# A two-layer transformer block: one more group by sevens in four down blocks, its combinations made earlier, and residuals added by transfers

## The chip, the cores and the metric

The kernel runs on one core of one Trainium2 chip. The metric is the device time of one execution in microseconds, lower is better. A core has five engines that run side by side, each with its own queue in order: TensorE (PE; its weight loads are shown as PEld), VectorE (DVE), ScalarE (ACT), GpSimd (POOL) and SyncE (SP). SP issues the plain loads, POOL the transfers that add to what lies at their destination; all run on 16 DMA engines.

## The reference

Two layers on 256 tokens of width 2048, each a mixer and an FFN. The change touches the FFN alone:

```python
def swiglu(hn, w_gate, w_up, w_down):
    return (jax.nn.silu(hn @ w_gate) * (hn @ w_up)) @ w_down

    for layer in range(DEPTH):
        ...
        h = h + swiglu(rmsnorm(h, ffn_norm[layer]), ffn_w_gate[layer], ffn_w_up[layer], ffn_w_down[layer])
    return rmsnorm(h, final_norm)
```

The FFN's inner width is 5632. Everything is float32. The kernel splits each operand of a matmul into a high part of type `F32R` and a rest of the same type, and a product is three matmuls: high by high, high by rest, rest by high.

## The kernel before

The inner width is cut into 11 pieces of 512 columns, and these into pieces of four, four and three. Each piece is first made by its gate/up blocks, one per 512 columns (called G0, G1, G2 and, in pieces of four, G3), and then used by two down blocks (D0, D1), each of which makes 1024 of the 2048 output columns for this piece. So a layer has 17 blocks, all written by `block` (L418).

A block multiplies 256 tokens (two halves `t`) by weights that come in units of 256 rows by 512 columns, 512 KB each. `load` (L166) has SP fetch a unit into a `raw` buffer. ScalarE casts the high part (`whi`, L179) and VectorE subtracts (`wlo`, L180). A unit is then 12 matmuls of 512 columns (lines L409 to L411), which add up in four PSUM banks `F[t][i]`.

Four units (two of rows, two of columns) make a group. A group that is done plainly takes 48 matmuls. A group in `comb` is done by sevens, which is Strassen's scheme in Winograd's form: the generator `seven` (L433) makes seven products of 6 matmuls in place of eight. For it, VectorE makes three sums of units (`total`, L384). ScalarE and VectorE split four tiles more (`halves`, L376 and L377). One sum is made by an adding load that POOL issues (L443). The tokens' side needs sums as well: `combine` (L387) makes them with VectorE and ScalarE, once per group and for all blocks that use it. At the end, `ends` (L460) recombines the products from the banks `M` into the buffer `e` (ScalarE at L462, four VectorE operations at L464).

Which groups go by sevens before the change: in gate/up blocks none or two of the four (`groups`); in D0 the first, in D1 of the pieces of four the first two, in D1 of the last piece the first. The combinations of `hid` for the down blocks are made by hooks: a hook `j` of a block runs before its plain unit `j`. In a piece of four, D0 makes the first at hook 4 and the second at hook 9. In the piece of three, G1 makes the only one at hook 6. `lead` says how many plain units come before the steps of the sevens begin to be mixed in.

At the end of a gate/up block VectorE and ScalarE form silu(gate) times up (L529 to L534). The result is transposed by TensorE in the next block's hook 2 (`turn`, L498), where ScalarE and VectorE write `hid` (L507, L508). At the end of a down block VectorE first makes `h +- e` in `e` (L554), which needs no accumulator, and then adds the four banks `F` to it into `h` (L561).

The order on each engine is not the code's: a planner sorts all instructions by the code's order as priority and by its own costs, so an instruction whose inputs are there can come tens of microseconds earlier than it is written. The buffers set how far an engine runs ahead: seven `raw` tiles, four `whi`, three `wlo`, two each of `thi`, `tlo` and `T`, four accumulator banks `F`, and one buffer `e`.

Of the kernel before, what the change touches and what calls it, by code (L numbers as in the profile page):

```python
# [16 lines left out]
NB = FF // 512  # L17
# [30 lines left out]
def body(tc, A, out):  # L48
# [364 lines left out]

    def sums():

        return [[mx.tile([128, 512], F32, name=f"e{t}{i}", tag=f"e{t}{i}", bufs=1) for i in range(2)] for t in range(2)]

    def block(src, x, comb, nd, hooks, tail=0, lead=2, trail=None):  # L418

# [38 lines left out]
            yield  # L458

        def ends():  # L460
            (c1, w5), (v, w7) = sums()
            S.copy(c1, M[0].t)  # L462
            for o, a, b, op in ((v, M[2], c1, ALU.subtract), (w5, M[1], v, ALU.add), (v, M[3], v, ALU.add), (w7, M[3], w5, ALU.add)):
                V.tensor_tensor(out=o, in0=a.t, in1=b, op=op)  # L464
            return [[c1, w5], [v, w7]]

        sevens = [s for m in comb for s in [seven(m)] for _ in range(7)]
        trail = trail or (3 if ns == 1 and nd > 3 else 2)
# [2 lines left out]
        for j, (i, u) in enumerate(plain):  # L471
# [14 lines left out]
            while k < len(sevens) and k < (j - lead + 2) * len(sevens) // gaps:  # L486
                next(sevens[k])
                k += 1
                if k == len(sevens):
                    e = ends()  # L490
        return [[y.t for y in f] for f in F], e

    def ffn(L, then, fin=None):

# [17 lines left out]
        for groups in ((0, 2, 2, 2), (2, 2, 2, 2), (2, 2, 2)):  # L512
            piece = len(groups)
            hid = ogp.tile([128, 16, 2, T], F32R, name="hid", tag="hid")
            late = {4: lambda hid=hid: ch.update({0: combine(hid[:, 0:4])})}
            for j in range(piece):
                hooks = {2: turn} if todo else {}
                if b == 0:
                    hooks[5] = lambda: cx.update({0: combine(X[:, 0:4])})
                    hooks[8] = rstd  # L520
                    hooks[10] = lambda: cx.update({1: combine(X[:, 4:8])})
                if j == 1 and piece == 3:

                    hooks[6] = late[4]
                F, e = block(lambda i, u: gu[b, u, i], lambda k: X[:, k], {m: lambda m=m: cx[m] for m in range(groups[j])}, 4, hooks)
                a = e or sums()
                for t in range(2):
                    if e:
                        V.tensor_tensor(out=a[t][0], in0=F[t][0], in1=e[t][0], op=(ALU.add, ALU.subtract)[t])  # L529
                    S.activation(a[t][0], a[t][0] if e else F[t][0], AF.Silu, scale=nrm["rs"][:, t:t + 1])  # L530
                for t in range(2):
                    if e:
                        V.tensor_tensor(out=a[t][1], in0=F[t][1], in1=e[t][1], op=ALU.add)
                    V.scalar_tensor_tensor(out=a[t][0], in0=a[t][1] if e else F[t][1], scalar=nrm["rs"][:, t:t + 1],  # L534
                                           in1=a[t][0], op0=ALU.mult, op1=ALU.mult)
                    todo.append((hid, j, t, a[t][0]))
                b += 1
            u0 = 2 * (b - piece)
            for p in range(2):
                end = b == NB and p == 1  # L540
                hooks = {2: turn} if todo else {}
                if p == 0 and piece == 4:
                    hooks.update(late)

                    hooks[9] = lambda hid=hid: ch.update({1: combine(hid[:, 4:8])})
                if end and fin:
                    hooks.update({5: lambda: then(0), 6: lambda: then(1)})
                last = (3, 1, 3) if end and fin else (0, 5 if 4 in hooks else 2)
                F, e = block(lambda i, u: dn[2 * p + i, u0 + u], lambda k: hid[:, k],
                             {m: lambda m=m: ch[m] for m in range(1 + (p == 1 and piece == 4))}, piece, hooks, *last)  # L550
                hs = [[h[:, t, (2 * p + i) * 512:(2 * p + i + 1) * 512] for i in range(2)] for t in range(2)]
                for t in range(2):
                    for i in range(2):
                        V.tensor_tensor(out=e[t][i], in0=hs[t][i], in1=e[t][i], op=ALU.subtract if t > i else ALU.add)  # L554
# [743 lines left out]
```

## Time and profile before

| | |
|---|---|
| median of 3 runs (lowest, highest) | 2227.39 us (2226.42, 2228.13) |
| the profiled execution | 2228.4 us, span 2226.6 us |
| granted clock of TensorE | 0.999 of full speed |
| TensorE busy | 2211.8 us, 99% of the span |
| VectorE busy | 1917.1 us, 86% |
| ScalarE busy | 1284.9 us, 58% |
| HBM reads | 447.58 MB |

The times in the rows are of the one profiled execution. Busy time counts an engine's compute instructions; where two of them overlap in the pipeline, the stretch counts once. One matmul is shown with the time that it takes from its start to its modelled end, and the next starts before that end. So the pace is read from the starts. Register, semaphore and issuing instructions are not busy time. A layer's FFN lies from about 440 to 1130 us (layer 0) and from about 1530 us to the end (layer 1).

### The profile page before, as it was taken

How to read it: one execution, taken by the hardware profiler on the slowest of the kernel's cores; microseconds unless marked ns; L12 is line 12 of the kernel's file. 1: busy time of each engine (PE TensorE's matmuls, PEld its weight loads, DVE VectorE, ACT ScalarE, POOL GpSimd, SP SyncE). 2: the span in 40 equal slices, each digit the busy share in tenths (PEclk: the TensorE clock that was granted, in tenths of full speed). 3: DMA queues.
4: the chain of work that ended last, by engine and by line, in shares of the span. 5: the costliest groups of instructions: out<-in, count | busy, mean ns of one | idle time of the engine just before them, and what ended most of it. 6: DMA issues, size and time to landing. Idle time of an engine off the chain costs nothing.

```text
span 2226.6 us, 30372 instructions
## 1 busy us (share of the span) xinstructions
PE 2211.8 (99%) x11002; PEld 1847.0 (83%) x11002; DVE 1917.1 (86%) x2713; ACT 1284.9 (58%) x1687; POOL 50.6 (2%) x62
## 2 busy tenths in 40 slices
PE   9999999999999999999999999999999999999998
PEld 8888888888888888888878888888888888888886
DVE  8899676679999999999966658866999999999998
ACT  6776664555555665555654444545665566555565
POOL 0000000000000000000000000000000000000000
PEclk9999999999999999999999999999999999999999
DMA  7445445677777776777665455556777777777774
GB/s 281 155 146 163 141 152 184 208 223 227 212 227 231 220 233 211 225 230 225 193 196 171 161 169 175 168 178 185 223 226 216 221 225 238 219 214 239 218 236 151
DMA packets 125992, 451.67 MB, mean 203 GB/s; under 512 B 14065, under 2 KB 15601, under 8 KB 125713
## 3 DMA queue, kind: packets, MB, share of 16 engines
q1 hardware_dynamic: 117488, 420.10, 58.3%
q0 software_dynamic: 8064, 29.36, 7.8%
q8 instruction: 86, 1.41, 0.3%
q14 instruction: 66, 0.53, 0.1%
q10 hardware_dynamic: 288, 0.27, 0.0%
HBM read 447.58 MB, written 2.10 MB: 202 GB/s over the span
## 4 chain that ended last, share of the span: by engine, by line
PE 95%; DVE 2%; issue 1%; ACT 1%; DMA 1%; DVEq 0%; ACTq 0%
PE F L411 15%; PE F L410 15%; PE F L409 15%; PE Pw L199 10%; PE Pw L204 5%; PE Px L303 5%; PE Px L304 5%; PE Px L305 5%; PE M L410 5%; PE M L411 4%; PE M L409 4%; PE Ph L503 1%; DVE wlo L180 1%; PE Psc L1068 1%; PE Pt L326 0%
## 5 line engine op out<-in xcount | busy, mean ns | idle before, releaser
L179 ACT CAST whi<-raw 128x1024 fp32r<-128x1024 f32 x720 | 755.3, 1051 | 666.8 <-PE F L411 263.8
L180 DVE TENSOR_TENSOR wlo<-raw,whi 128x1024 fp32r<-128x1024 f32 x720 | 874.5, 1219 | 189.3 <-PE Px L304 70.1
L199 PE MATMUL Pw<-X,whi 128*128 128x512 f32 x1088 | 388.3, 400 | 0.0
L409 PE MATMUL F<-whi,X 128*128 128x512 f32 x848 | 331.4, 391 | 0.0
L410 PE MATMUL F<-wlo,X 128*128 128x512 f32 x848 | 330.4, 390 | 0.0
L411 PE MATMUL F<-whi,X 128*128 128x512 f32 x848 | 330.0, 389 | 0.0
L204 PE MATMUL Pw<-X,wlo 128*128 128x256 f32 x1088 | 304.8, 280 | 1.0 <-DVE wlo L180 0.9
L376 ACT CAST thi<-T 128x1024 fp32r<-128x1024 f32 x168 | 176.6, 1051 | 124.1 <-DVE T L384 84.0
L199 PEld LDWEIGHTS Pw<-X,whi 128*128 128x128 f32 x1088 | 204.2, 188 | 47.7 <-issue 0.5
L377 DVE TENSOR_TENSOR tlo<-T,thi 128x1024 fp32r<-128x1024 f32 x168 | 205.1, 1221 | 28.0 <-ACT thi L376 27.3
L204 PEld LDWEIGHTS Pw<-X,wlo 128*128 128x128 f32 x1088 | 205.3, 189 | 2.4 <-DVE wlo L180 2.0
L409 PE MATMUL F<-whi,hid 128*128 128x512 f32 x480 | 187.5, 391 | 0.0
L411 PE MATMUL F<-whi,hid 128*128 128x512 f32 x480 | 186.9, 389 | 0.0
L410 PE MATMUL F<-wlo,hid 128*128 128x512 f32 x480 | 186.8, 389 | 0.0
L411 PEld LDWEIGHTS F<-whi,X 128*128 128x128 f32 x848 | 159.2, 188 | 33.1
L409 PEld LDWEIGHTS F<-whi,X 128*128 128x128 f32 x848 | 159.2, 188 | 32.7
L410 PEld LDWEIGHTS F<-wlo,X 128*128 128x128 f32 x848 | 159.2, 188 | 32.4
L384 DVE TENSOR_TENSOR T<-T,raw 128x1024 f32<-128x1024 f32 x112 | 136.5, 1219 | 1.1 <-DMA raw<-in_gu 0.2
L410 PE MATMUL M<-tlo,comb 128*128 128x512 f32 x336 | 131.8, 392 | 1.1 <-DVE tlo L377 1.0
L409 PE MATMUL M<-thi,comb 128*128 128x512 f32 x336 | 131.4, 391 | 0.0
L411 PE MATMUL M<-thi,comb 128*128 128x512 f32 x336 | 130.9, 390 | 0.0
L411 PEld LDWEIGHTS F<-whi,hid 128*128 128x128 f32 x480 | 90.1, 188 | 18.8
(389 smaller groups left out, 3409.5 us busy)
## 6 DMA issues: line engine op xcount, KB each, us to landing
raw<-in_gu SPq DMA_DIRECT2D x352, 512.0 KB, 4.4
raw<-in_dn SPq DMA_DIRECT2D x176, 512.0 KB, 4.4
raw<-in_w0w SPq DMA_DIRECT2D x72, 512.0 KB, 3.6
raw<-in_wo SPq DMA_DIRECT2D x64, 512.0 KB, 3.6
raw<-in_w1w SPq DMA_DIRECT2D x64, 512.0 KB, 3.6
raw<-in_gu POOLq DMA_DIRECT2D x40, 512.0 KB, 6.8
raw<-in_w1x SPq DMA_DIRECT2D x32, 512.0 KB, 3.7
raw<-in_w0x SPq DMA_DIRECT2D x16, 512.0 KB, 3.6
```

The lines of the kernel that those rows point to most:

```text
L179: S.copy(hi, raw)
L180: V.tensor_sub(lo, raw, hi.bitcast(F32))
L199: PE.matmul(P.rearrange("p a b -> p (a b)"), hi[:, kk], X[:, k].rearrange("p a b -> p (a b)"), start=k == 0, stop=False)
L204: PE.matmul(P[:, 0], lo[:, kk], X[:, k, 0], start=False, stop=k == NK - 1)
L303: PE.matmul(Ps[t], x[:, 0, ts], hi[:, kk], start=k == 0, stop=False)
L304: PE.matmul(Ps[t], x[:, 0, ts], lo[:, kk], start=False, stop=False)
L376: S.copy(hi, t)
L377: V.tensor_sub(lo, t, hi.bitcast(F32))
L384: V.tensor_tensor(out=t, in0=a, in1=b, op=ALU.add)
L409: PE.matmul(self.t, xh, hi[:, kk], start=self.i == kk == 0, stop=False)
L410: PE.matmul(self.t, xh, lo[:, kk], start=False, stop=False)
L411: PE.matmul(self.t, xl, hi[:, kk], start=False, stop=kk == 1 and self.i == self.n - 1)
```

## The change

In the pieces of four, D0 gets its second group by sevens, as D1 had it. Both combinations are now made in the gate/up blocks: the first at hook 6 of G2, the second at hook 6 of G3 (`chs`). D0 then has no hook 4, so its `lead` becomes 2, the value that D1 has. In all down blocks but those of the last piece (`b < NB`) the residual is no longer added by VectorE: it adds the banks `F` to `e`, and POOL issues two transfers that add the halves of `e` onto `h` in SBUF, 512 KB each. For this the four tiles of `e` become one tile of the same size.

```diff
     def sums():
-        return [[mx.tile([128, 512], F32, name=f"e{t}{i}", tag=f"e{t}{i}", bufs=1) for i in range(2)] for t in range(2)]
+        e = mx.tile([128, 2, 2, 512], F32, name="e", tag="e", bufs=1)
+        return [[e[:, t, i] for i in range(2)] for t in range(2)], e
...
         def ends():
-            (c1, w5), (v, w7) = sums()
+            ((c1, w5), (v, w7)), e = sums()
...
-            return [[c1, w5], [v, w7]]
+            return [[c1, w5], [v, w7]], e
...
-            late = {4: lambda hid=hid: ch.update({0: combine(hid[:, 0:4])})}
+            both = piece == 4
+            chs = lambda m, hid=hid: lambda: ch.update({m: combine(hid[:, 4 * m:4 * m + 4])})
...
-                if j == 1 and piece == 3:
-                    hooks[6] = late[4]
+                if j == 1 and piece == 3 or j == 2 and both:
+                    hooks[6] = chs(0)
+                if j == 3 and both:
+                    hooks[6] = chs(1)
...
-                if p == 0 and piece == 4:
-                    hooks.update(late)
-                    hooks[9] = lambda hid=hid: ch.update({1: combine(hid[:, 4:8])})
+                if p == 0 and piece == 4 and not both:
+                    hooks[4] = chs(0)
+                    hooks[9] = chs(1)
...
-                             {m: lambda m=m: ch[m] for m in range(1 + (p == 1 and piece == 4))}, piece, hooks, *last)
+                             {m: lambda m=m: ch[m] for m in range(1 + (both or p == 1 and piece == 4))}, piece, hooks, *last)
...
+                if b < NB:
+                    for t in range(2):
+                        for i in range(2):
+                            V.tensor_tensor(out=e[t][i], in0=F[t][i], in1=e[t][i], op=ALU.subtract if t > i else ALU.add)
+                        G.dma_start(h[:, t, 2 * p * 512:(2 * p + 2) * 512], es[:, t].rearrange("p a b -> p (a b)"), accum_op=ALU.add)
+                    continue
```

## Rows read from the trace of the kernel before

**Rows 1.** The page of the whole span: its length, and the busy time, the share of the span and the instructions of TensorE and VectorE.

```profile
span 2226.6 us, 30372 instructions
...
PE 2211.8 (99%) x11002; PEld 1847.0 (83%) x11002; DVE 1917.1 (86%) x2713; ACT 1284.9 (58%) x1687; POOL 50.6 (2%) x62
```

**Rows 2.** Busy time of each engine in eight stretches, each one block of an FFN layer, cut where the last VectorE instruction of the block before and of this block ends. Columns: stretch (us), its length, then busy us and instructions of PE, PEld, DVE, ACT and POOL, the granted clock, the share of the 16 DMA engines' time in use, GB/s. In order: layer 0's first piece of four, G3, D0 and D1; G0 of its second piece; G0 and G1 of its last piece; layer 1, G0 of the second piece and G0 of the last.

```profile
564.90:607.00 42.10, 42.02 (x189) 34.33 (x188) 41.03 (x46) 24.65 (x27) 0.95 (x2) 1.00 0.70 223
607.00:646.70 39.70, 39.70 (x181) 32.97 (x180) 37.57 (x44) 21.44 (x23) 1.64 (x2) 1.00 0.73 209
646.70:688.00 41.30, 41.30 (x184) 34.15 (x183) 38.57 (x40) 22.55 (x24) 0.96 (x2) 1.00 0.77 231
688.00:730.10 42.10, 42.10 (x186) 34.29 (x185) 39.84 (x40) 24.84 (x26) 2.49 (x3) 1.00 0.81 233
938.50:982.90 44.40, 43.64 (x193) 35.56 (x192) 41.94 (x42) 26.68 (x28) 2.48 (x3) 1.00 0.79 228
982.90:1024.80 41.90, 41.90 (x191) 34.76 (x190) 40.96 (x46) 25.24 (x28) 1.73 (x2) 1.00 0.73 217
1780.00:1822.40 42.40, 42.17 (x186) 34.23 (x185) 39.88 (x41) 24.90 (x26) 2.57 (x3) 1.00 0.80 230
2031.00:2074.20 43.20, 43.20 (x192) 35.48 (x191) 41.96 (x42) 26.51 (x28) 2.50 (x3) 1.00 0.80 233
```

**Rows 3.** TensorE's matmuls in order of time in that D1; first and last of 33 that follow each other. Columns: start, duration, engine, line, operation, output and inputs, shape, count.

```profile
654.74 0.39 PE L410 MATMUL F<-wlo,comb 128*128 128x512 f32 x1
...
662.00 0.39 PE L409 MATMUL M<-thi,comb 128*128 128x512 f32 x1
```

**Rows 4.** Who waited for whom over the whole span, weight loads of TensorE: total us, times, longest.

```profile
PEld M L410 <- DVE tlo L377: 4.0, 8, 1.2
```

**Rows 5.** VectorE's instructions in order of time at the start of that G3 (columns as in group 3; x2 merges two that follow each other).

```profile
559.46 0.68 DVE L529 TENSOR_TENSOR e<-F,e 128x512 f32<-128x512 f32 x1
560.06 0.68 DVE L533 TENSOR_TENSOR e<-F,e 128x512 f32<-128x512 f32 x1
...
567.12 2.35 DVE L180 TENSOR_TENSOR wlo<-raw,whi 128x1024 fp32r<-128x1024 f32 x2
569.39 1.22 DVE L384 TENSOR_TENSOR T<-T,raw 128x1024 f32<-128x1024 f32 x1
...
576.27 1.22 DVE L392 TENSOR_TENSOR cf<-hid 128x1024 f32<-128x1024 f32 x1
```

**Rows 6.** Groups of instructions by line, engine, operation and shape over the whole span: count, busy us, mean ns of one, idle time of the engine before them and what ended it.

```profile
L376 ACT CAST thi<-T 128x1024 fp32r<-128x1024 f32 x168 | 176.6, 1051 | 124.1 <-DVE T L384 84.0 <-PE F L410 23.1 <-PE F L411 14.3
...
L554 DVE TENSOR_TENSOR e<-h,e 128x512 f32<-128x512 f32 x48 | 31.2, 682 | 0.0
```

**Rows 7.** VectorE's instructions in order of time in G1 of layer 0's last piece, parts of one combination: its first operation (L392), two of its four small ones (L395) with what follows each.

```profile
994.28 1.22 DVE L392 TENSOR_TENSOR cf<-hid 128x1024 f32<-128x1024 f32 x1
...
1009.50 0.41 DVE L395 TENSOR_TENSOR cc<-cf 128x256 f32<-128x256 f32 x1
1009.83 1.21 DVE L377 TENSOR_TENSOR tlo<-raw,thi 128x1024 fp32r<-128x1024 f32 x1
...
1014.23 0.87 DVE L395 TENSOR_TENSOR cc<-cf,cc 128x256 f32<-128x256 f32 x2
1015.29 1.23 DVE L180 TENSOR_TENSOR wlo<-raw,whi 128x1024 fp32r<-128x1024 f32 x1 [0.19 <-PE F L410]
```

**Rows 8.** The DMA view of the whole span: packets, MB and share of the 16 engines' time of the two queues (q1 is what SP issues, q0 what POOL issues), then issues with the engine that issues, their count, KB each and median us from issue to landing.

```profile
q1 hardware_dynamic: 117488, 420.10, 58.3%
q0 software_dynamic: 8064, 29.36, 7.8%
...
raw<-in_dn SPq DMA_DIRECT2D x176, 512.0 KB, 4.4
...
raw<-in_gu POOLq DMA_DIRECT2D x40, 512.0 KB, 6.8
...
raw<-in_dn POOLq DMA_DIRECT2D x16, 512.0 KB, 7.3
```

**Rows 9.** ScalarE's instructions in order of time: in the D1 at 646.7 the first that writes the block's buffer `e`, in the G0 at 688.0 the one that reads the sum that the adding load made.

```profile
667.79 0.58 ACT L462 COPY e<-M 128x512 f32<-128x512 f32 x1
...
700.35 1.06 ACT L376 CAST thi<-raw 128x1024 fp32r<-128x1024 f32 x1 [0.79 <-PE M L411]
```

**Rows 10.** POOL's instructions in order of time around that D1, and in G0 of layer 0's last piece: each issues one adding load.

```profile
641.04 0.86 POOL L443 DMA_DIRECT2D raw<-in_dn  x1 [33.26 <-DVE T L384]
656.93 0.86 POOL L443 DMA_DIRECT2D raw<-in_dn  x1 [15.03 <-ACT thi L376]
687.90 0.86 POOL L443 DMA_DIRECT2D raw<-in_gu  x1 [30.11 <-ACT whi L179]
700.08 0.86 POOL L443 DMA_DIRECT2D raw<-in_gu  x1 [11.32 <-ACT thi L376]
...
950.57 0.86 POOL L443 DMA_DIRECT2D raw<-in_gu  x1 [11.32 <-ACT thi L376]
```

**Rows 11.** The chain of work that ended last, in order of time, two pieces of it in G0 of layer 0's last piece: start, us, what.

```profile
951.20 9.00 DMA raw<-in_gu
960.28 1.06 ACT whi L179
```

**Rows 12.** Who waited for whom over the whole span, ScalarE for weight loads of gate and up.

```profile
ACT whi L179 <- DMA raw<-in_gu: 18.4, 15, 2.1
```

More of the change, by code (lines that the diff above doesn't have):

```diff
@@ L490, in block @@
                     e = ends()
-        return [[y.t for y in f] for f in F], e
+        return [[y.t for y in f] for f in F], *(e or (None, None))
     def ffn(L, then, fin=None):
@@ L521, in ffn @@
                     hooks[10] = lambda: cx.update({1: combine(X[:, 4:8])})
-                if j == 1 and piece == 3:
-                    hooks[6] = late[4]
-                F, e = block(lambda i, u: gu[b, u, i], lambda k: X[:, k], {m: lambda m=m: cx[m] for m in range(groups[j])}, 4, hooks)
-                a = e or sums()
+                if j == 1 and piece == 3 or j == 2 and both:
+                    hooks[6] = chs(0)
+                if j == 3 and both:
+                    hooks[6] = chs(1)
+                F, e, _ = block(lambda i, u: gu[b, u, i], lambda k: X[:, k], {m: lambda m=m: cx[m] for m in range(groups[j])}, 4, hooks)
+                a = e or sums()[0]
                 for t in range(2):
@@ L548, in ffn @@
                 last = (3, 1, 3) if end and fin else (0, 5 if 4 in hooks else 2)
-                F, e = block(lambda i, u: dn[2 * p + i, u0 + u], lambda k: hid[:, k],
-                             {m: lambda m=m: ch[m] for m in range(1 + (p == 1 and piece == 4))}, piece, hooks, *last)
+                F, e, es = block(lambda i, u: dn[2 * p + i, u0 + u], lambda k: hid[:, k],
+                             {m: lambda m=m: ch[m] for m in range(1 + (both or p == 1 and piece == 4))}, piece, hooks, *last)
                 hs = [[h[:, t, (2 * p + i) * 512:(2 * p + i + 1) * 512] for i in range(2)] for t in range(2)]
+                if b < NB:
[4 more added lines that the diff above has]
+                    continue
                 for t in range(2):
```

## The prediction

> **What bounds the kernel now.** I read the page's busy times first [rows 1]: TensorE 99% of the span and VectorE 86%, so the order of these two decides. Then I cut the two FFN layers into blocks at the end of each block's last VectorE instruction and read the busy times block by block [rows 2]. Call a piece's gate/up blocks G0 to G3 and its down blocks D0 and D1. TensorE is busy in all of a D0 (39.70 of 39.70 us) and of a D1 (41.30 of 41.30), at a granted clock of 1.00, the 2.4 GHz level. VectorE is close behind: 37.57 us in a D0, 38.57 in a D1, 41.03 in a G3. So a matmul taken away is worth its own time only as long as VectorE, which gets work in exchange, stays under TensorE. The third view is the matmuls in order of time [rows 3]: 32 starts of 128x512 between 654.74 and 662.00 us, 0.2269 us each. This pace, and not the 0.39 us of one, prices a matmul. A fourth view, who waited for whom, says what TensorE loses to VectorE in all: the largest entry is 4.0 us in 8 waits of the weight load on `tlo` [rows 4]. So hardly more than the matmuls themselves is there to be won.
>
> **Part 1, the second group by sevens.** A plain group of D0 is 4 units of 12 matmuls, 48; by sevens it is 7 steps of 6, 42. Four D0 blocks (two per layer) lose 6 each: 24 x 0.2269 = 5.45 us, all on the engine that is never idle there. This is the whole gain.
>
> What pays for it. On VectorE a plain group is 4 subtractions (L180); by sevens it is 3 of these, 4 of L377 and 3 sums of L384, 10 in all, so 6 more. Two 1024-element instructions back to back start 1.135 us apart (567.12 and 569.39 are two apart [rows 5]), so a D0 gets 6.8 us more. ScalarE gets 3 more casts of 1.05 us (L376 [rows 6]) and is busy in 21.44 of a D0's 39.70 us [rows 2], so that is hidden. Loads stay 16 per block (12+4 becomes 8+8), and there is one more adding load (L443).
>
> **Part 2, the combinations move** from D0 (hooks 4 and 9) to hook 6 of G2 and G3. One `combine` is two 1024-element operations (2.27 us) and four of 256, 0.33 us apart where one is followed by another engine's input and 0.43 where they are in a chain [rows 7]: 3.8 us. The count stays, so this is a question of place. The order in the trace is not the order in the code: the first operation on `hid` runs at 576.27 [rows 5], in a G3, though the code puts it in the D0 whose window begins at 607.0. So G3 carries a combination already and only G2 gets a new one. VectorE's need in a gate block with two groups by sevens: 28 operations of 1.135 us (31.8), 10 of 512 elements at 0.60 (559.46 to 560.06 [rows 5]) for the recombination, the end and the turn, two scaled ones of about 0.66, together 39.1 us. TensorE needs 180 x 0.2269 + 0.9 for the 8 transposes, 41.7. With a combination VectorE needs 42.9, 1.2 more than TensorE has. Bounds: nothing, because G1 of a last piece, which has a combination at hook 6 and two groups by sevens, shows TensorE busy for 41.90 of 41.90 us [rows 2]; and 1.2 us in each of the eight G2 and G3, 9.6 us, if no tile is ready ahead. I take the nearest rows: idle 0.08 us in the G3 (42.10 less 42.02) and nothing in that G1, mean 0.04. With the new D0, which has the form of such a gate block, that is eight blocks, four G2 and four D0: 0.3 us. The start of D0 loses the three extra plain units that `lead` 5 gave; the turn at hook 2 then has 42 matmuls ahead of it in place of 24, which is more cover, not less.
>
> **Part 3, the residual.** In the eight down blocks of the pieces of four, the four operations `h +- e` (L554, 682 ns [rows 6], 0.60 in a row) go: 2.4 us of VectorE per block. The four after the last matmul stay, with `e` as their output in place of `h`, so accumulator banks come free when they did. D0's VectorE need becomes 28 x 1.135 + 10 x 0.60 = 37.8 us for 41.7 of TensorE. So D0 stays under TensorE by 3.9 us, and over a layer VectorE has 2 x 6.8 - 4 x 2.4 = 4.0 us more while rows 2 show 0.9 to 2.7 us idle in each block. What VectorE saves here gives no time back by itself, because it isn't the bound there.
>
> In place of these come two additions of 512 KB from SBUF onto `h` per block end, 16 in all, on the POOL queue. The trace has none of this kind. The nearest is the adding load L443: 7.3 us to landing, against 4.4 for a plain load [rows 8]. In time of all 16 engines: queue 0 took 7.8% of 2226.6 us for 29.36 MB, so 3.1 us per 512 KB; queue 1 took 58.3% for 420.10 MB, 1.62 us. A D1 then has 16 x 1.62 + 2 x 3.1 = 32.1 us of transfers in 41.3, 0.78; the row says 0.77. With two additions it is 38.3, 0.93. So it fits on average, and it is tight for some 12 us after each block end.
>
> Who waits for that? The buffer `e` is written again by the next block's L462, at 667.79 for a D0 that ended at 646.7 [rows 9]: 21 us, against two issues of 0.86 and two additions, 7.3 + 3.1. `h` is read next in the last piece. Behind the additions on the POOL queue stands the next block's adding load. From D0 to D1 the first is issued at 641.04, before D0's end, and the second at 656.93; from D1 to G0 at 687.90 and 700.08 [rows 10], the first of them just when the additions become ready. If it comes behind them it is late by up to 2 x 0.86 + 6.2 = 7.9 us; its reader at 700.35 [rows 9] leaves 12.4 less the 6.8 to landing [rows 8], 5.6. And the weight loads beside them become slow: in a G0 the chain of waits passes through a load of 9.00 us that was issued just behind an adding load [rows 10, 11], and TensorE is idle in that block for 0.76 us (44.40 less 43.64 [rows 2]). The four G0 that follow a D1 give 0, 0.76, 0.23 and 0: mean 0.25 us. Bounds for a block end: less than nothing is possible (VectorE has 2.4 us less to do there, which could take away the idle time of the four G0, 0.99 in all); from above, two additions' 6.2 us less what is ready ahead (the second rival). I take the mean of the four rows, since these are the blocks in which adding loads stand closest: 8 x 0.25 = 2.0 us.
>
> The Trainium skill, DMA: Bandwidth & Descriptors, section Issuing engines are not separate DMA queues, speaks against this part: what is issued from GpSimd runs on the same 16 engines as SP's loads and interleaves with them. By that the additions are no free path, and the 9.00 us load agrees. The Trainium skill's fit for one transfer (same title, section Anatomy of one DMA), 2.0 us and the bytes by 436 GB/s, would give 3.2 us for an addition, an estimate; by it the 2.0 us above would be nothing and the sum 2222.2. The adding loads here took 6.8 and 7.3 [rows 8], so the fit does not hold in this crowd.
>
> **The sum.** -5.45 + 0.3 + 2.0 = -3.15 us. The profiled execution took 2228.4 us, 1.8 of it around the span of 2226.6, and lies 1.0 above the median of 2227.39; it becomes 2225.2, and the median 2224.2. Its own range: 2222.9 to 2226.
>
> **Rivals.** *The gain comes whole.* The additions hide, as the D1 with 0.77 of the transfers' time in use hides two adding loads, and the 2.4 us that VectorE saves at each end clears the G0: -5.45 - 0.5 = -6, so 2221.4; with the 0.3 and half of the 2.0 still 2222.9. For it: the margins above. Against: the transfers are 0.80 busy in a G0 already.
>
> *The transfers become the bound after each down block.* Place: the 12.2 us between the two adding loads of a block (687.90 to 700.08). In them 16/41.3 x 12.2 = 4.7 loads are due, 7.7 us of transfers, with 3.1 for the adding load and 6.2 for the additions 17.0: 4.8 us too much. TensorE lives on from the three `wlo` tiles, at least 6 matmuls each, 4.1 us; with two of them 2.7. What is left is 0.7 to 2.1 us per end, 1.4 in the middle: 8 x 1.4 = 11.2, and 2227.4 - 5.45 + 0.3 + 11.2 = 2233.4, slower. From 1.2 us per end on it is slower by over 0.2%. For it: the 9.00 us load, and ScalarE's 18.4 us of waiting on such loads [rows 12]. Against: that load cost 0.76.
>
> *VectorE becomes the bound in G2 and G3*, two blocks in a row, 1.2 us each: 4 x 2.4 = 9.6, of which the tiles ahead cover one block's share, 4.8. -5.45 + 4.8 + 2.0 = +1.4: 2228.8, no change. Against: the G3 at 564.9 has a combination, and the D0 behind it, which by the code has two, shows TensorE busy throughout [rows 2].
>
> *It does not do what it says:* the planner puts the combinations elsewhere; the 5.45 us stay in any case, since the matmuls go.
>
> **How the numbers follow.** Forecast 0.42, gain whole 0.31, transfers 0.15, VectorE 0.12. A change of 0.2% (4.5 us) is about what a measurement of this kernel can tell from none. Faster than 2222.9: the whole gain and a tenth of the forecast, 0.35. Slower than 2231.9: most of the transfers' case and a little of VectorE's, 0.16. The rest, 0.49, is within. For 8 in 10 the range goes from 2221.0 (whole gain and scatter) to 2232.0, into the transfers' case.
>
> **What would show it.** TensorE: 24 matmuls fewer, and D0 windows shorter by 1.4 us. VectorE: L554's operation in the last pieces alone, 16 times in place of 48, and about 4 us more work per layer. POOL: 60 adding loads in place of 56, and 16 additions. Wrong if plain loads beside the additions stay near 4.4 us (then faster), if ScalarE's waits on DMA grow by more than some 10 us or G0 and D1 show over 1 us idle (slower), or if the additions land in other times than 7 to 10 us.

## The result, and the profile after

The changed kernel takes 2243.11 us (2241.97 to 2244.55, 6 runs) beside 2227.21 (2226.42 to 2228.13) for the kernel before: ratio 1.007, 95% interval 1.0058 to 1.0082, so 15.9 us slower. Forecast were 2224.2 and a range to 2232.0. First the page, in the lines that answer to [rows 1]:

```profile
span 2242.0 us, 30343 instructions
...
PE 2216.6 (99%) x10978; PEld 1841.9 (82%) x10978; DVE 1922.2 (86%) x2705; ACT 1295.5 (58%) x1699; POOL 68.0 (3%) x82
...
PE 91%; DVE 3%; DMA 3%; ACT 1%; issue 1%; DVEq 0%; ACTq 0%; SPq 0%
```

The 24 matmuls are gone (11002 to 10978) and POOL has its 20 instructions more. VectorE's busy time rose by only 5 us. The last line gives shares of the chain of work that ended last: DMA has 3% of it (1% before), though the median plain load in the DMA view is hardly slower: 4.4 us for gate and up as before, 4.6 for down in place of 4.4. TensorE's busy time still reads 99%: it rose by 4.8 us with 24 matmuls fewer, so a part of what is lost counts as busy. So one has to go to the blocks. In the windows (columns as in [rows 2]), D0, D1 and G0 of layer 0 that follow the first piece's gate blocks, and then the D1 and G0 at the end of the second piece:

```profile
603.30:645.50 42.20, 41.51 (x185) 33.41 (x184) 40.34 (x41) 24.90 (x26) 3.45 (x4) 1.00 0.82 236
645.50:686.90 41.40, 41.40 (x182) 33.70 (x181) 39.79 (x40) 24.01 (x25) 3.47 (x4) 1.00 0.87 255
686.90:733.70 46.80, 44.80 (x196) 36.50 (x196) 39.71 (x40) 25.04 (x26) 2.60 (x3) 1.00 0.81 236
899.60:945.10 45.50, 42.49 (x179) 34.22 (x178) 38.45 (x39) 23.92 (x24) 4.33 (x5) 0.96 0.82 229
945.10:989.20 44.10, 43.55 (x193) 35.65 (x192) 40.92 (x41) 25.69 (x27) 2.60 (x3) 1.00 0.88 255
```

TensorE is now idle in these blocks: 0.69 us in the D0 (42.20 less 41.51), 2.00 in the first G0, 3.01 in the second D1; in [rows 2] a D0, a D1 and a G0 in a row had nothing idle. VectorE is never full for a whole block (40.34 of 42.20, 38.45 of 45.50). Who waited for whom, over the whole span:

```profile
ACT whi L179 <- DMA raw<-in_dn: 31.3, 15, 4.9
...
ACT whi L179 <- DMA raw<-in_gu: 25.8, 16, 4.9
...
DVE T L384 <- DMA raw<-in_gu: 18.1, 10, 4.0
...
PEld M L410 <- DVE tlo L377: 11.9, 12, 3.4
...
PEld M L409 <- ACT thi L376: 10.6, 23, 1.7
```

ScalarE's waits on loads of the gate blocks grew from 18.4 us [rows 12] to 25.8, and there is a new entry, 31.3 us on loads of the down blocks. The wait of TensorE's weight loads on `tlo` went from 4.0 us [rows 4] to 11.9. So weights come late. The chain of waits at the start of the D1 at 899.6 shows one such case (start, us, what):

```profile
900.83 10.08 DMA raw<-in_dn
...
911.00 0.10 DVE T L384
...
912.14 1.23 DVE tlo L377
```

and POOL's and TensorE's instructions beside it:

```profile
897.98 0.86 POOL L561 DMA_DIRECT2D h<-e  x1 [23.30 <-DVE e L560]
899.93 0.86 POOL L561 DMA_DIRECT2D h<-e  x1 [1.09 <-DVE e L560]
901.31 0.87 POOL L444 DMA_DIRECT2D raw<-in_dn  x1 [0.52 <-DVE T L384]
```

```profile
910.02 0.39 PE L409 MATMUL M<-thi,comb 128*128 128x512 f32 x1
913.41 0.50 PE L410 MATMUL M<-tlo,comb 128*128 128x512 f32 x1 [3.01 <-DVE tlo L377]
```

A weight load issued at 900.83, beside both additions (L561) and the adding load (L444), needs 10.08 us; the sum `T` waits for it, then `tlo`, then TensorE, which starts nothing from 910.02 to 913.41.

To compare kernels I use one measure, called **stalls**: over successive matmul starts, the sum of what each gap exceeds the pace of its shape (0.2265 us for 512 columns), block by block, cut as in [rows 2]. In the two FFNs, without G0 of the first piece of each layer:

| us | G1 to G3 | D0 | D1 | G0 | sum |
|---|---|---|---|---|---|
| before | 3.2 | 0.5 | 0.6 | 2.2 | 6.5 |
| after | 4.3 | 5.2 | 11.5 | 5.6 | 26.6 |

26.6 less 6.5 is 20.1; less the 5.45 us of the matmuls saved it is 14.6, of the 15.4 us by which the span grew. So the loss lies in D0, D1 and G0.

### The profile page after: what moved, and what is told of

Same layout as the page of the kernel before. It is cut to its first block, busy times and chain, and to the rows that moved or that the text cites. A ratio compares the mean times of both kernels' runs of the same rounds, so it can differ in the third digit from the quotient of the medians.

```text
span 2242.0 us, 30343 instructions
## 1 busy us (share of the span) xinstructions
PE 2216.6 (99%) x10978; PEld 1841.9 (82%) x10978; DVE 1922.2 (86%) x2705; ACT 1295.5 (58%) x1699; POOL 68.0 (3%) x82
## 3 DMA queue, kind: packets, MB, share of 16 engines
q0 software_dynamic: 10944, 39.85, 10.5%
## 4 chain that ended last, share of the span: by engine, by line
PE 91%; DVE 3%; DMA 3%; ACT 1%; issue 1%; DVEq 0%; ACTq 0%; SPq 0%
PE F L409 14%; PE F L410 14%; PE F L411 14%; PE Pw L199 10%; PE Pw L204 5%; PE Px L303 5%; PE M L410 5%; PE Px L305 5%; PE Px L304 5%; PE M L409 5%; PE M L411 4%; DMA raw<-in_dn 2%; DVE wlo L180 1%; PE Ph L504 1%; DVE tlo L377 1%
## 5 line engine op out<-in xcount | busy, mean ns | idle before, releaser
L376 ACT CAST thi<-T 128x1024 fp32r<-128x1024 f32 x180 | 189.3, 1051 | 148.7 <-DVE T L384 101.4
L377 DVE TENSOR_TENSOR tlo<-T,thi 128x1024 fp32r<-128x1024 f32 x180 | 219.5, 1220 | 20.1 <-ACT thi L376 19.7
L410 PE MATMUL F<-wlo,hid 128*128 128x512 f32 x424 | 166.8, 393 | 0.0
L409 PE MATMUL F<-whi,hid 128*128 128x512 f32 x424 | 166.4, 394 | 0.0
L411 PE MATMUL F<-whi,hid 128*128 128x512 f32 x424 | 166.1, 392 | 0.0
L410 PE MATMUL M<-tlo,comb 128*128 128x512 f32 x360 | 142.2, 395 | 7.5 <-DVE tlo L377 7.4
L384 DVE TENSOR_TENSOR T<-T,raw 128x1024 f32<-128x1024 f32 x120 | 146.1, 1218 | 0.6
L409 PE MATMUL M<-thi,comb 128*128 128x512 f32 x360 | 142.5, 396 | 4.3 <-ACT thi L376 4.2
L411 PE MATMUL M<-thi,comb 128*128 128x512 f32 x360 | 140.6, 391 | 0.0
L410 PEld LDWEIGHTS F<-wlo,hid 128*128 128x128 f32 x424 | 80.3, 189 | 17.5 <-DVE wlo L180 1.1
```

The costliest lines, as they stand in the source:

```text
L376: S.copy(hi, t)
L377: V.tensor_sub(lo, t, hi.bitcast(F32))
L384: V.tensor_tensor(out=t, in0=a, in1=b, op=ALU.add)
L409: PE.matmul(self.t, xh, hi[:, kk], start=self.i == kk == 0, stop=False)
L410: PE.matmul(self.t, xh, lo[:, kk], start=False, stop=False)
L411: PE.matmul(self.t, xl, hi[:, kk], start=False, stop=kk == 1 and self.i == self.n - 1)
```

## The experiments

Differences are to the kernel before, run beside them on the same chip (2227.6 to 2228.6 us). Lines are those of the changed kernel, unless a diff shows otherwise.

**The three parts alone.** `move_only`: combinations in G2 and G3, D0 with one group and `lead` 2, residual on VectorE. `sevens_only`: the changed kernel with the residual on VectorE. `adds_only`: the kernel before with the additions by transfers. `move_only` has both of these edits and `sevens_only` the second alone; `adds_only` has the first alone, and its combinations are made at hooks 4 and 9 of D0 as before. The lines are cut:

```diff
-  {m: lambda m=m: ch[m] for m in range(1 + (both or p == 1 and piece == 4))}   # move_only, adds_only
+  {m: lambda m=m: ch[m] for m in range(1 + (p == 1 and piece == 4))}
-  G.dma_start(h[...], es[...], accum_op=ALU.add)                               # move_only, sevens_only
+  V.tensor_tensor(out=hs[t][i], in0=F[t][i], in1=e[t][i], op=ALU.add)          # with h +- e before it
```

> The combinations made in G2 and G3, D0 with one group by sevens and lead 2 (it has no hook 4), residual on VectorE: no matmul is saved. Both theories in part: if VectorE's combination in G2 costs what the bound of 1.2 us per block says, 2232 to 2237; if the tiles ahead cover it, 2226 to 2229. What the second group costs by itself is then this run against the one with the second group.

> The second group by sevens and the moved combinations alone: all down blocks add the residual on VectorE as before. Theory A: 24 matmuls of 0.2269 us less 5.4 us, against 1.2 us of waiting in each D0, so about 2227, and not over 2229. Theory B: 2236 or more. If the waiting in D0 is also due to the additions, 2223.

> The additions onto h by transfers alone: D0 has one group by sevens, and its combinations at hooks 4 and 9, as before. Theory A (the additions' transfer time makes the weight loads after each down block late): most of the loss is here, 8 to 14 us over the kernel before, 2235 to 2241, with idle TensorE at the start of D1 and of the G0 behind a D1. Theory B (the second group by sevens and the moved combinations cost the time, through VectorE and the planner's order): VectorE only gets less work here, so 2226 to 2229.

Measured: `move_only` 2229.61 (ratio 1.0004, 0.9994 to 1.0013): moved by themselves, the combinations cost nothing. `sevens_only` 2252.44 (1.0109, 1.0094 to 1.0124), 23.9 us slower, with stalls of 33.7 spread over all kinds of block. It differs from `move_only` by the second group in D0 alone, so that group turned a move that was free into a loss. `adds_only` 2257.67 (1.013, 1.0115 to 1.0145), 29.1 slower and beyond what I expected, with 21.5 of its 30.8 us of stalls in D1. Each of these last two is worse alone than both together (15.9). They do not add up, so this could not yet name the cause.

**Copies in place of additions, and half of them.**

```diff
-  G.dma_start(h[...], es[...], accum_op=ALU.add)
+  G.dma_start(h[...], es[...])                                # copy_not_add
-  G.dma_start(...)                                            # half_adds: for t = 1 by VectorE, e by F, then h by e
+  if t == 0: G.dma_start(...)
+  else: V.tensor_tensor(out=hs[t][i], in0=hs[t][i], in1=e[t][i], op=ALU.add)
```

> The changed kernel with the 16 transfers onto h as plain copies in place of additions, from the same queue: the residual of the down blocks of the pieces of four is left out of the output. If the adding (3.1 us of all 16 engines for 512 KB against 1.6) is what makes loads late, about half of the loss at the block ends goes: 2234 to 2238. If any two transfers more at that place do it, 2241 to 2244. If it is the POOL queue alone, 2241 to 2244 too, with loads no faster.

> The changed kernel with the addition by transfer for the first token half alone; the second half is added on VectorE (two operations of 0.6 us more per down block). If the loss goes with the transfers' bytes: 2233 to 2238. If it is only the second of two additions that is too much, as the loads have 3 to 8 us in hand: 2229 to 2232. If VectorE's work counts as much as the transfers: 2243 or over.

Measured: copies 2233.28 (1.0021, 1.0011 to 1.003), half of the additions 2242.2 (1.0066, 1.0051 to 1.0081). With the same 16 transfers of the same size, copies (with no residual, so the sum onto `h` is missing) give back 11 of the 16 us; half of the additions, with 16 operations more for VectorE, gives back 1. G0's stalls were 0.0 with copies.

**No transfers at all.** The `G.dma_start` of L561 is left out.

> The changed kernel with the residual of the pieces of four left out altogether: no transfer onto h and no addition by VectorE; VectorE, ScalarE and the matmuls are those of the changed kernel. With 3.1 us of all engines per transfer it took 2243.1, with 1.5 (the copies) 2233.3. Theory A (the transfers' own time): the last step gives about as much again per microsecond, the stalls of D1 and G0 fall to about 1, 2225 to 2229, and D0's 5 to 8 us stay. Rival (what counts is any transfer beside the loads, or VectorE's order): 2232 to 2234.

Measured: 2232.52 (1.0022, 1.0012 to 1.0031), the time of the copies. So my reading "so much per microsecond of transfer" fell: a copy costs nothing that can be measured, an addition all of it.

The run also prices VectorE's time. `sevens_only` differs from `no_transfers` by the 32 operations `h +- e` alone, 17 us of VectorE's busy time (1939.7 less 1922.7), and lies 23.9 us above the kernel before where `no_transfers` lies 4.8 above it. So in the changed kernel what VectorE does at the end of a down block costs about its full time, though VectorE is busy for 86% of the span.

The DMA views of the changed kernel, of `copy_not_add` and of `no_transfers` (columns as in [rows 8]):

```profile
q0 software_dynamic: 10944, 39.85, 10.5%
...
raw<-in_dn SPq DMA_DIRECT2D x176, 512.0 KB, 4.6
...
h<-e POOLq DMA_DIRECT2D x16, 512.0 KB, 7.8
```

```profile
q0 software_dynamic: 10944, 39.85, 9.4%
...
h<-e POOLq DMA_DIRECT2D x16, 512.0 KB, 5.0
```

```profile
q0 software_dynamic: 8640, 31.46, 8.5%
```

Packets and bytes of the first two are the same. In time of all engines, the 16 additions took (10.5% of 2242.0 less 8.5% of 2228.5) / 16 = 2.9 us each, the copies (9.4% of 2233.7 less the same) / 16 = 1.3. The median of the plain loads (4.6) says little of it. At the end of the first D0, where no adding load stands between them, the three plain loads behind the first transfer took 8.43, 6.04 and 6.21 us with additions (issued at 646.69 to 651.24) and 5.77, 6.43 and 4.80 with copies (646.64 to 651.82). Over all eight ends, the 28 plain loads issued in the 8 us behind the first transfer took 7.4 us in the median with additions, 5.1 with copies. Where an adding load comes on top, as in the D1 at 899.6 of the changed kernel, the three issued from 900.83 to 906.25 took 8.3 to 10.1.

**Additions by GpSimd.** `tensor_tensor` on POOL adds `e` onto `h` in place of the transfers.

> The changed kernel with the 16 additions done by GpSimd's own arithmetic (h + e, 128x1024 each) in place of transfers; VectorE's work is that of the changed kernel. If the additions' transfers are what makes D1 and G0 wait (16 us of idle TensorE there, 2 before): 2228 to 2233, D0's waits remaining. If GpSimd's two inputs from SBUF hold up VectorE's for their length, VectorE loses what it saved and more: 2240 or over.

Measured: 2261.37 (1.015, 1.0134 to 1.0165), the worst of all. VectorE's and POOL's instructions in order of time at the end of a D0:

```profile
645.93 0.69 DVE L560 TENSOR_TENSOR e<-F,e 128x512 f32<-128x512 f32 x1
646.54 2.84 DVE L180 TENSOR_TENSOR wlo<-raw,whi 128x1024 fp32r<-128x1024 f32 x1
649.29 3.43 DVE L377 TENSOR_TENSOR tlo<-T,thi 128x1024 fp32r<-128x1024 f32 x1
652.65 1.21 DVE L180 TENSOR_TENSOR wlo<-raw,whi 128x1024 fp32r<-128x1024 f32 x1
```

```profile
644.97 6.67 POOL L562 TENSOR_TENSOR h<-h,e 128x1024 f32<-128x1024 f32 x2 [5.71 <-DVE e L560]
```

The two VectorE instructions that read two SBUF tiles and begin while POOL adds take 2.84 and 3.43 us in place of 1.21. L560, which reads one operand from PSUM, keeps its 0.69. VectorE's busy time rises to 1952.7 us. So this is no free engine either.

**Where the raw buffers go.** Seven `raw` buffers lie in two pools of three and four. `b12` is held longest (for the sum, the adding load and `halves`); here it always comes from the pool of four.

```diff
-        if more and loads[0] > 0 and loads[0] % 7 in (1, 3, 5, 6):
+        others[0] += not hold
+        if more and loads[0] > 0 and (hold or others[0] % 5 in (1, 3)):
...
-            b12 = load(src(1, 2 * m))
+            b12 = load(src(1, 2 * m), True)
```

> The changed kernel with another choice of raw buffers: the unit that an adding load completes (b12, held some 20 us) always takes one of the four raw4 buffers, and the others take raw4 two times in five, so no two long-held units crowd one tag. If the waits in D0 come from loads that SP issues late because such a unit holds the next buffer: D0's idle time falls from about 1.2 us to under 0.4 each and the time to 2234 to 2239. If D0 waits because VectorE has too much to do there: 2242 to 2245.

> The same choice of raw buffers in the kernel before, the control. It waits for 0.1 to 1 us per block there, so 2225 to 2228 if held buffers matter, 2227 to 2230 if not; any loss here says that the choice itself is worse.

> The kernel before with the buffer rule of before_hold, again, in five rounds, for a smaller interval: the first time was 2224.7, 2.8 us below before. If that was real, 2224 to 2226 with an interval below 1; the stalls of G0 and G3 in its FFNs are 2.8 us less than before, so not lower than 2224.

Measured: on the changed kernel 2240.77 (1.006, 1.0044 to 1.0077), 2.7 us less than without the rule, with D0's stalls at 9.3: no cure. On the kernel before 2224.71 (0.9986, 0.9977 to 0.9996) and, again, 2223.44 (0.9983, 0.9974 to 0.9991): a gain of its own of 2.8 and 4.1 us, with stalls of 3.4 and 3.2 in place of 6.5.

**Spreading D0, and later additions.** `d0_spread` gives the D0 of pieces of four `lead` and `trail` 1; `spread_hold` adds the buffer rule; `adds_late` writes the additions at hook 3 of the next block.

```diff
-  last = (3, 1, 3) if end and fin else (0, 5 if 4 in hooks else 2)
+  last = (3, 1, 3) if end and fin else (0, 1, 1) if p == 0 and both else (0, 5 if 4 in hooks else 2)
```

> The changed kernel with lead and trail of 1 in the D0 blocks of the pieces of four, so that the seven steps of the two groups are spread over more of the block; the transfers stay. Theory A (the additions make the loads late, in D1 and G0): the 17 us of stalls in D1 and G0 stay; 2240 to 2244. Theory B (D0's own crowding is a loss of its own: adding loads 12.8 us apart, VectorE without a gap): the 5.2 us of stalls in D0 fall below 2, 2237 to 2241.

> The changed kernel with d0_spread's spreading and the buffer rule of after_hold (the unit that is held longest always in the four-buffer pool). If D0's waits come from its crowding and its loads from buffers that are held long, D0's stalls fall from 5.2 to about 1 and those of D1 and G0 stay above 8: 2234 to 2238. If the additions also make D0 late, 2240 as in after_hold.

> The changed kernel with the two additions of a block end issued at hook 3 of the next block, some 10 us later, in place of at once. If what hurts is that the additions stand beside the adding load and the plain loads of a block's first 12 us, the stalls of D1 and G0 (17 us) fall by half, 2233 to 2237, provided that e is free before the next block's L463 writes it. If the transfers are too much wherever they stand, 2240 to 2246; if e is free too late, TensorE waits in the middle of D1 and G0 and it is slower than 2246.

Measured: 2251.24 (1.0104, 1.0089 to 1.012), 2246.09 (1.0078, 1.0065 to 1.0092) and 2244.85 (1.0077, 1.0063 to 1.0091); the first two are above what I expected. `d0_spread` left D0's stalls at 5.8 and raised D1's to 19.2, which I did not trace to a cause. It tells nothing of whether D0's steps being close together hurts, since the planner hardly spread them: in the first D0 the second adding load comes 13.4 us after the first (605.68, 619.03) in place of 12.8. `adds_late` tells nothing of its question either: the planner issued the additions as early as before (646.29, ahead of the D0's end at 647.73, for 644.09).

**Combinations earlier, left out, and both left out.** `early_combos` puts them at hook 6 of G1 and G2. `no_combos` makes none in the pieces of four and uses `cx[m]` in their place. `neither` is that without the transfers too.

```diff
-                if j == 1 and piece == 3 or j == 2 and both:        # early_combos
+                if j == 1:
-                if j == 3 and both:
+                if j == 2 and both:
```

> The changed kernel with the combinations one block earlier, at hook 6 of G1 and G2 in place of G2 and G3. Theory (D0 waits because VectorE comes out of G2 and G3 with nothing ahead): VectorE's idle time in G3 rises from 0.5 to 1.1 us as in the kernel before, and D0's stalls fall from 5.2 to below 3; 2239 to 2242. Rival (D0's own 28 operations and loads are tight in any case): D0 stays at 5 to 6, 2242 to 2244.

> The changed kernel with the combinations of hid left out in the pieces of four (the down blocks use those of the gate blocks' tokens in their place, so their products are others): VectorE has 7.6 us less per piece, in G2 and G3. If VectorE's being full there is the cause of D0's waits, D0's stalls fall from 5.2 to about 1 and those of D1 and G0 by a part, 2234 to 2239. If D0 is tight by itself, they stay at 4 to 6 and the time at 2240 to 2243.

> Both left out: no transfers and no residual in the pieces of four, and no combinations of hid there. What is left of the change is its 24 matmuls less. If theories A and B name all of the loss, the stalls in the FFNs fall to about 6 us as in the kernel before and the time is 2221 to 2224; if it stays above 2226, something else in the second group by sevens costs time.

Measured: 2238.25 (1.0045, 1.003 to 1.006), 2231.53 (1.0014, 1.0005 to 1.0024) and 2220.24 (0.9965, 0.9952 to 0.9978), each somewhat below what I expected. Together with the changed kernel and `no_transfers` this is a table of two by two, in us to before:

| | combinations made | left out |
|---|---|---|
| additions by transfers | +15.9 | +3.8 |
| no transfers | +4.8 | -7.5 |

The transfers cost 11.1 and 11.3 us, the combinations 12.1 and 12.3: here, in the time, the two causes do add up. The table leaves the residual out where it has no transfers; on VectorE it costs 19 us (`sevens_only` beside `no_transfers`), more than as transfers. By blocks, D0 has its stalls only where combinations are made (5.2 and 5.8 us, else 0.7), G0 only where there are transfers (5.6 and 7.0, else 0.0 and 0.5); D1's 11.5 need both (4.1 without combinations, 3.5 without transfers, 1.0 without either). Without both, the page shows the gain of the matmuls whole:

```profile
span 2219.9 us, 30310 instructions
...
PE 2206.2 (99%) x10978; PEld 1843.2 (83%) x10978; DVE 1897.4 (85%) x2657; ACT 1289.3 (58%) x1691; POOL 54.0 (2%) x66
```

**What the combinations cost: VectorE's time or two buffers.** `combine` takes VectorE, but `cf` and `cc` also take the two `T` buffers, and `total` needs one of them for every group by sevens. In `after_inplace` both lie in the result tile instead, as F32R, so that the rest part of the combinations comes out as zero; VectorE's operations keep their number and sizes. The diff is cut (casts of type left out). `sevens_inplace` has that, the residual on VectorE, and the buffer rule of `before_hold`.

```diff
-        f = mx.tile([128, 4, T], F32, name="cf", tag="T", bufs=2)
-        c = mx.tile([128, 4, 2, 128], F32, name="cc4", tag="T", bufs=2)
         r = fp.tile([128, 2, 4, 2, 128], F32R, name="comb", tag="comb", bufs=4)
+        f = r[:, 0].rearrange("p a b c -> p a (b c)")
+        c = r[:, 1]
```

> The changed kernel with combine working inside its own result tile: cf and cc no longer take the two T buffers, which the sums of the sevens need as well. VectorE's instructions and their sizes stay; the intermediate values are rounded to F32R there, so the rest part of the combinations is left out (zero). Leaving the combinations out gave 11.6 us of the loss back. If what they cost was the T buffers (a total that waits for one), this gives about as much: 2230 to 2236. If it was VectorE's time in G2 and G3, nothing changes: 2240 to 2244.

> The second group by sevens with VectorE's residual (sevens_only), the combinations inside their result tile as in after_inplace, and the buffer rule of before_hold; no transfers onto h. VectorE has 2.4 us more per down block than in the changed kernel and no combination less. If VectorE's time is the cause, it stays slow as sevens_only did with 2252: 2240 to 2252. If the T buffers were, it comes below the kernel before: 2221 to 2228.

Measured: 2236.42 (1.0038, 1.0023 to 1.0053) and 2223.12 (0.9976, 0.9966 to 0.9986). In place alone gives 7.2 of the 12 us back: D0's stalls fall from 5.2 to 0.5 and D1's from 11.5 to 4.8, while those of G1 to G3 rise from 4.3 to 9.4. `sevens_inplace` is some 28 us faster than `sevens_only` (each against the kernel before beside it), with the same VectorE work, and 4.6 faster than the kernel before. The kernel before with the same buffer rule is 2.8 and 4.1 faster, so of these 4.6 us only 0.5 to 1.8 are left for the second group, and the intervals overlap. VectorE in order of time at the end of a G3 shows what moves. The changed kernel:

```profile
578.92 1.22 DVE L392 TENSOR_TENSOR cf<-hid 128x1024 f32<-128x1024 f32 x1
...
598.92 1.22 DVE L397 TENSOR_TENSOR comb<-cc,comb 128x1024 fp32r<-128x1024 f32 x1
...
601.87 1.41 DVE L538 SCALAR_TENSOR_TENSOR e<-e,rs 128x512 f32<-128x512 f32 x2
...
605.46 1.21 DVE L384 TENSOR_TENSOR T<-raw,raw 128x1024 f32<-128x1024 f32 x1
```

and `after_inplace`:

```profile
598.54 1.23 DVE L384 TENSOR_TENSOR T<-raw,raw 128x1024 f32<-128x1024 f32 x1 [0.21 <-DMA raw<-in_dn]
...
608.56 0.75 DVE L538 SCALAR_TENSOR_TENSOR e<-e,rs 128x512 f32<-128x512 f32 x1
```

L538 is the last VectorE instruction of G3. In the changed kernel `cf` holds one `T` buffer from 578.92 and `cc` the other until 600.14, and D0's first sum `T<-raw,raw` comes 2.2 us after the end of G3 (605.46 less 603.28); in place, it comes 10.8 us ahead of that end (609.31 less 598.54). The trace doesn't show the sum waiting for a buffer: both are free for 5.3 us before it runs, and its place behind G3's end is the planner's order. That the two buffers set this place is shown by taking them away. It holds in all four D0: the sum comes 2.2 us behind G3's end in the changed kernel, `copy_not_add` and `no_transfers` (D0's stalls 5.2, 8.1 and 5.8), 9.8 to 11.0 ahead in place (0.5), 11.9 ahead in `no_combos` (0.7). The adding load must wait for that sum, since the sum reads `b12` before it is overwritten. POOL's instructions of the changed kernel, then of `after_inplace`:

```profile
607.21 0.86 POOL L444 DMA_DIRECT2D raw<-in_dn  x1 [30.22 <-DVE T L384]
619.99 0.86 POOL L444 DMA_DIRECT2D raw<-in_dn  x1 [11.93 <-DVE T L384]
```

```profile
600.29 0.86 POOL L444 DMA_DIRECT2D raw<-in_dn  x1 [28.50 <-DMA raw<-in_dn]
617.78 0.86 POOL L444 DMA_DIRECT2D raw<-in_dn  x1 [16.63 <-ACT thi L376]
```

So in the changed kernel the two groups crowd in D0: their adding loads are issued 12.8 us apart for 17.5. What follows in its chain of waits and on ScalarE:

```profile
621.73 1.15 DVE tlo L377
...
622.90 5.92 DMA raw<-in_dn
```

```profile
628.89 1.05 ACT L179 CAST whi<-raw 128x1024 fp32r<-128x1024 f32 x1 [4.43 <-DMA raw<-in_dn]
```

`tlo` (L377) frees the buffer of `b12`, only then does SP issue the next load, and ScalarE waits 4.43 us for it. This happens in D0 before any addition has run.

## Why the prediction was wrong

**The 5.45 us were right** as a price of the matmuls: 24 went, and with both costs away the time is 7.5 us lower (`neither`). In a kernel that makes its combinations and adds its residual they were not got: `sevens_inplace` is 4.6 us faster than the kernel before, but 0.5 to 1.8 of that is all that its buffer rule does not give by itself. The rival *gain whole* had 2221.4 for the case that nothing stands against it. (Its second sum is off: with the 0.3 and half of the 2.0 it gives 2223.2, not 2222.9.)

**The step "eight blocks x 0.04 = 0.3 us" failed**: beside the new group by sevens the combinations cost some 12 us, not 0.3, and 7.2 of that by the two buffers that they borrow. I asked of a moved combination only how much VectorE time it takes and whether a block has room for it. I did not ask which buffers it holds. The section on the kernel before lists "two each of `thi`, `tlo` and `T`", and the code has `cf` and `cc` on tag `T` (L389, L390). In the kernel before and in `move_only`, D0 has one group by sevens and three groups of plain units to live on, and there a late first sum does no harm: in `move_only` it runs 3.3 us after the end of G3, later than in the changed kernel, and D0's stalls are 0.9. VectorE's instructions there:

```profile
603.79 1.41 DVE L538 SCALAR_TENSOR_TENSOR e<-e,rs 128x512 f32<-128x512 f32 x2
...
608.51 1.22 DVE L384 TENSOR_TENSOR T<-raw,raw 128x1024 f32<-128x1024 f32 x1
```

The nearest rows, a G3 and a G1 with combinations, were right for their blocks and did not carry over to a D0 with two groups.

**The step "8 ends x 0.25 = 2.0 us" failed in its size**: about 11 us, 1.4 per end in the mean. That is the middle of the rival *The transfers become the bound after each down block* (1.4 per end, 11.2 us), by its mechanism: loads beside the additions late, then `T`, `tlo` and TensorE. That the middle was met is luck: the rival priced the stretch behind a D1, and most of the stalls lie behind a D0, where the late sums add to them. I gave it 0.15. Its rows were there (the 9.00 us load [rows 11], DMA share 0.80 in G0 [rows 2]); against it I set that the one late load had cost only 0.76 us, which says that a margin was not yet used up, not that there is more. The Trainium skill, DMA: Bandwidth & Descriptors, section Issuing engines are not separate DMA queues, cited against this part, agrees with the 10.08 us load; I cited it and then priced the part without it. The rule gives no price, since copies on the same queue cost nothing. The estimate of an addition's engine time (3.1 us) came out at 2.9, and the median landing at 7.8 in the 7 to 10 that I gave. The point of decision, 1.2 us per end, fell as predicted on the slower side. But the rival's time of 2233.4 lacked the second cost.

**VectorE becomes the bound in G2 and G3**: not there. G1 to G3 have 4.3 us of stalls for 3.2 before. `sevens_inplace` has all of that work and 2.4 us more per down block, TensorE's stalls are 6.5 us in all as in the kernel before (3.2 with the same buffer rule), and VectorE's busy time is the highest of all these kernels but `pool_adds`:

```profile
span 2221.5 us, 30342 instructions
...
PE 2207.4 (99%) x10978; PEld 1842.2 (83%) x10978; DVE 1940.0 (87%) x2737; ACT 1297.0 (58%) x1699; POOL 54.0 (2%) x66
```

So "D0 stays under TensorE by 3.9 us" was true, and not what mattered.

**The step "What VectorE saves here gives no time back by itself" failed for the kernel as it was built**: there the 2.4 us per down block are worth some 19 us in all (`sevens_only` beside `no_transfers`), of which the transfers take back 11. So the third part, given the other two, gained 8 us. With the combinations in place and the buffer rule (`sevens_inplace`) VectorE has this time to spare, and the third part isn't needed.

**It does not do what it says**: it did. L565, the operation that was L554 [rows 6], runs 16 times in place of 48, and the signs that I had named for "slower" (ScalarE's waits grown by over 10 us, G0 and D1 with over 1 us idle) are all there. D0 windows did not become shorter by 1.4 us: the first is 42.20 us for 39.70.

**What stays open.** In place alone gave 7.2 us, leaving the combinations out 12.1 with the transfers; the other 5 may be VectorE's time, or the stalls of 4.9 us that `after_inplace` has in the G3 of each layer's first piece, taken together (0.8 in the changed kernel), which I did not trace to a cause. That the rest part is zero in place is a difference that no run took apart either. Why an addition makes the loads beside it late and a copy does not is argued from its 2.9 us of all engines for 1.3, and not tested further; the price per addition isn't even: with half of them done by VectorE 1 us came back, with none done at all 11. `sevens_inplace` differs from `sevens_only` by the buffer rule too, and the two were not run apart. That `adds_only` is worse than the changed kernel (D1 21.5 for 11.5) fits with `cf` and `cc` holding `T` in D0, just ahead of the additions, but no run tested it. And `combine` with the full rest part and without the `T` buffers was not made; it needs another place for `cf` and `cc`, 4 KB each in a partition by their shapes.

## What to carry to other kernels

When a step is moved or a second one of its kind is added, list the buffers that it holds and from when to when, not only its time on its engine: here two borrowed buffers cost more than the matmuls saved. A transfer that adds is not a copy: price it by the engine time of adding transfers in the trace and ask what the loads beside it have as a margin. An engine that is idle for 14% of the span need not have that time to spare where it counts. When parts do not add up alone, take away the suspected costs two by two; here that left nothing of the loss. And set a run that holds two edits beside a control that holds one of them.

## What the runs showed of the hardware

**The clock after a stall.** After TensorE had started nothing from 910.02 to 913.41, its matmuls ran for 3.4 us at the lower level. The windows of the changed kernel:

```profile
908.00:914.80 6.80, 3.79 (x17) 2.84 (x16) 3.80 (x4) 1.64 (x2) 0.87 (x1) 1.00 0.74 219
914.80:918.20 3.40, 3.40 (x10) 2.63 (x9) 3.12 (x4) 2.48 (x3) 0.00 (x0) 0.51 0.97 199
918.20:920.00 1.80, 1.80 (x10) 1.46 (x9) 1.80 (x3) 0.46 (x1) 0.00 (x0) 1.00 1.01 412
```

The granted clock is 0.51 in the middle stretch, the 1.2 GHz level, and its matmuls are 0.43 us apart in the chain of waits for 0.23 before and after: about eight of them, some 1.6 us lost on top of the stall, half as much again. It is not so after each stall of this length: in `d0_spread` TensorE starts nothing from 916.92 to 920.38, and the granted clock stays at 1.00:

```profile
917.00:920.40 3.40, 0.33 (x3) 0.02 (x1) 0.85 (x2) 2.06 (x3) 0.00 (x0) 1.00 1.06 366
920.40:924.00 3.60, 3.60 (x16) 2.98 (x17) 3.16 (x3) 1.94 (x2) 0.00 (x0) 1.00 1.00 298
```

**An adding transfer from SBUF to SBUF** of 512 KB took 2.9 us of all 16 engines, a copy of the same 1.3, with the same packets and bytes.

**GpSimd and VectorE**: beside a GpSimd addition of two SBUF tiles (3.36 us each), the VectorE instructions that read two SBUF tiles and began during it took 2.84 and 3.43 us for 1.21. The Trainium skill, GPSIMD Engine Reference, section 1. Specifications, names such a contention for VectorE instructions with two SBUF inputs; the trace of `pool_adds` agrees, also in that the one with a PSUM operand kept its time.
